# Windowed attention of two heads at a time on the halves of the TensorE array

## The chip, the cores and the metric

The kernel runs on one core of a Trainium2 chip. The metric is the device time of one execution in microseconds (us); smaller is better. TensorE multiplies matrices (its records are PE for the products and PEld for the loading of weights), VectorE is DVE, ScalarE is ACT, GpSimd is POOL, and SyncE (SP) issues most of the DMAs.

## The reference: two layers of a hybrid trunk

The reference runs two layers over 128 context tokens and 1024 sample tokens of 1024 channels. Layer 0 has state-space heads beside long convolutions. Layer 1, which the change touches, is attention with 16 heads of 64 channels. Context tokens attend to all context tokens. The sample is a grid of 16 rows of 64 tokens; each sample token attends to a window of 8 rows by 16 columns with a learned bias, and inside the same softmax to 128 cached keys:

```python
s_loc = jnp.einsum('bhrqd,bhrikd->bhrqik', q, k_rows).astype(jnp.float32) * (HD_C ** -0.5)
...
s_loc = s_loc + bias.transpose(0, 1, 3, 2, 4)[None].astype(jnp.float32)
s_loc = jnp.where(col_in[:, None, :], s_loc, -jnp.inf)
s_ctx = jnp.einsum('bhrqd,bhkd->bhrqk', q, ck).astype(jnp.float32) * (HD_C ** -0.5)
s = jnp.concatenate([s_loc.reshape(b, H_C, R, GRID_W, kh * GRID_W), s_ctx], axis=-1)
p = jax.nn.softmax(s, axis=-1).astype(v.dtype)
...
o = jnp.einsum('bhrqik,bhrikd->bhrqd', p_loc, v_rows) + jnp.einsum('bhrqk,bhkd->bhrqd', p_ctx, cv)
o = o.transpose(0, 2, 3, 1, 4).reshape(b, L, D_C)
return (o * jax.nn.silu(g)) @ w_out
```

## The kernel before

**Foreground and background.** The projections are the foreground: `proj` (L148) multiplies one chunk of 128 output channels with all tokens, in three blocks of 386 columns, each of 8 row blocks times three products (high times high, high times low, low times high: operands are split into a rounded part of type F32R and the rest). `v_proj` (L1164, products L1175 to L1177) does the values with 256 columns. After every block, `tick` (L90) adds `rate` to a credit and lets the background generators in `self.bg` run for as many steps (one step is up to the next `yield`) as the credit allows. In layer 1 the rate is `RA` (L47, 3.9). The time between two ticks is called a slot in the prediction: 24 products of the projection, then the background's steps.

**Order.** `qkv` (L1192) goes over the eight pairs of heads j. It projects the pair's queries `qt` and keys `kt`, for every second j the values of four heads, and puts `attn(j)` into the background. After that come eight chunks of the gates (`silu2`), each multiplied with the attention's output of its pair, and then the output projection (`final`). Semaphores are set by a planner from the data that instructions share. It also orders each engine's and each queue's instructions by when it reckons them ready, so that the order need not be that of the code.

**One attention before** (`attn`, L1258). It loads the cached keys `ck`, the cached values `cv` and the windowed values `vw` (16 DMAs). Then for each of the two heads it makes operands of 128 rows for a head of 64 channels: `Q` holds the queries' rounded part in the head's own 64 rows and the rest in the other 64 (L1285, L1286); `KH` and `KL` hold the keys' rounded part and the rest in the head's own rows (L1290 to L1293) and a copy of them in the other rows (L1294, L1295). So one product of 128 rows with `KH` and one with `KL` (L1320, L1321) give all four products of the parts.

The tiles follow: one tile of 128 context queries for each head, then for each head eight tiles of 128 sample queries (8 grid rows by 16 columns) against 512 keys, four groups of 128. They pass three stages, one stage later with each round of the loop: scores and softmax; the transposition of the four 128 by 128 blocks of weights through TensorE (L1329) and a copy out of PSUM to `Pt` (L1331); the products with the values (L1348), four of them, whose output is 64 channels, and so takes the half of the array's columns, and of the output tile `O`, that belongs to the head. A product of plain f32 operands appears as two records in the trace, a product of F32R operands and a transposition as one. There is a yield after the first and the second stage.

`softmax` (L1240) adds the bias table `Tb` to the scores and finds the maximum in one VectorE instruction (L1251), takes the exponential with its sum on ScalarE (L1253), and divides on VectorE (L1254, L1255). The tables of a head (two tiles of 128 by 3 by 512, one for the upper and one for the lower half of the queries) are loaded by 16 DMAs when the head's first sample tile comes up (`load_tables`, L1155).

**Buffers.** PSUM has five banks for the background (`p_bg`, L198) and three for projections (`p_pj`). `Q`, `KH` and `KL` have two buffers each, `sz` three, `Pt` two, `ck` and `cv` two, `vw` and the tables one.

## Time and profile before

| | us |
|---|---|
| median of 3 runs | 2197.95 (2196.88 to 2198.25) |
| profiled execution, first to last instruction | 2195.9 |
| TensorE busy (products) | 2156.0 |
| VectorE busy | 1423.3 |
| ScalarE busy | 995.3 |
| value products of the attention (L1348), first and last start | 1456.2 and 2067.4 |

The profile is of one execution; the profiler gives its span from the first to the last instruction, and no further time of its own. A row of the trace in order of time gives the start, the duration, the engine, the line, the operation, output and inputs, rows and columns of the array in use (64*128 is 64 rows and 128 columns), the shape that is streamed and how many neighbouring instructions were merged into the row. A row of a list by line gives the number of instructions, their busy time and the mean of one in ns, and behind the second bar the engine's idle time before them with what ended it. Records of TensorE overlap, since products are pipelined: what one costs is the time from its start to the next one's start.

### The profile page before, as it was taken

The numbers are of one execution on the slowest core, as the hardware profiler recorded it, in microseconds if no ns is written. First come the engines' busy times: TensorE is split into PE (matmuls) and PEld (weight loads), VectorE is DVE, ScalarE is ACT, GpSimd is POOL, SyncE is SP. The second block draws the span as 40 slices with busy tenths as digits, with TensorE's granted clock in tenths as the row PEclk, the third lists the DMA queues.
The fourth block names the chain that finished last, engine by engine and source line by source line (L and its number), as shares of the span: only waits on it lengthen the run. The fifth ranks groups of instructions, "written<-read, shape, count | busy, mean of one in ns | idle before, by whom it ended". The sixth has DMA issues, their size and how long they took to land.

```text
span 2195.9 us, 34064 instructions
## 1 busy us (share of the span) xinstructions
PE 2156.0 (98%) x13024; PEld 1937.6 (88%) x13024; DVE 1423.3 (65%) x2948; ACT 995.3 (45%) x2119; POOL 125.4 (6%) x241
## 2 busy tenths in 40 slices
PE   7999999999999999999999999999999999999998
PEld 3899998889999999888878999998888888888877
DVE  5798755546778778987888855734453544555474
ACT  3576544452333232545557303644554544554331
POOL 1110000110000000000000000200000000000000
PEclk9999999999999999999999999999999999999999
DMA  8142255764211122433342521522222223244352
GB/s 322 44 131 98 101 190 179 219 205 156 88 66 63 57 106 86 162 107 119 116 148 96 180 91 49 145 86 60 78 85 81 66 82 94 70 123 126 105 207 78
DMA packets 114947, 256.22 MB, mean 117 GB/s; under 512 B 27048, under 2 KB 63420, under 8 KB 112320
## 3 DMA queue, kind: packets, MB, share of 16 engines
q1 hardware_dynamic: 99472, 191.38, 27.6%
q0 software_dynamic: 15312, 62.67, 8.0%
q8 instruction: 103, 1.69, 0.3%
q14 instruction: 60, 0.48, 0.1%
HBM read 186.61 MB, written 67.38 MB: 116 GB/s over the span
## 4 chain that ended last, share of the span: by engine, by line
PE 58%; issue 2%; DVE 2%; DMA 1%; ACT 1%; POOLq 0%; POOL 0%; SPq 0%; ACTq 0%; DVEq 0%
PE pj L158 9%; PE pj L159 9%; PE pj L160 9%; PE bg L1348 6%; PE bg L1329 3%; PE bg L1320 2%; PE pj L1175 2%; PE pj L1176 2%; PE pj L1177 2%; PE bg L1321 1%; PE bg L1037 1%; PE bg L1005 1%; PE pj L1375 1%; PE pj L1373 1%; PE pj L1374 1%
## 5 line engine op out<-in xcount | busy, mean ns | idle before, releaser
L158 PE MATMUL pj<-hh,whi 128*128 128x386 f32 x1728 | 600.4, 347 | 0.5 <-DVE acc L862 0.5
L159 PE MATMUL pj<-hl,whi 128*128 128x386 f32 x1728 | 591.4, 342 | 0.0
L160 PE MATMUL pj<-hh,wlo 128*128 128x386 f32 x1728 | 588.6, 341 | 0.0
L158 PEld LDWEIGHTS pj<-hh,whi 128*128 128x128 f32 x1728 | 326.4, 189 | 11.5 <-issue 5.7
L159 PEld LDWEIGHTS pj<-hl,whi 128*128 128x128 f32 x1728 | 326.8, 189 | 9.8 <-issue 6.5
L160 PEld LDWEIGHTS pj<-hh,wlo 128*128 128x128 f32 x1728 | 326.6, 189 | 3.5 <-issue 3.1
L131 DVE TENSOR_TENSOR wlo<-wraw,whi 128x1024 fp32r<-128x1024 f32 x108 | 131.9, 1222 | 138.9 <-ACT whi L130 132.1
L130 ACT CAST whi<-wraw 128x1024 fp32r<-128x1024 f32 x108 | 113.0, 1048 | 233.2 <-PE pj L159 225.7
L1251 DVE CUSTOM_DVE_ANT_0 sz<-bg,Tb 128x512 f32<-128x512 f32 x128 | 88.1, 689 | 166.9 <-PE bg L1321 159.6
L598 ACT COPY raw<-pj 128x386 f32<-128x386 f32 x105 | 50.5, 483 | 169.4 <-PE pj L160 82.8
L1331 ACT COPY Pt<-bg 128x512 f32<-128x512 f32 (+1 forms) x144 | 79.0, 549 | 97.1 <-PE bg L1329 95.6
L1253 ACT ACTIVATE sz<-sz,mx 128x512 f32<-128x512 f32 x128 | 92.7, 724 | 53.9 <-DVE mx L1251 53.5
L159 PE MATMUL pj<-ylo,whi 128*128 128x386 f32 x324 | 111.0, 343 | 0.0
L160 PE MATMUL pj<-yhi,wlo 128*128 128x386 f32 x324 | 110.5, 341 | 0.0
L158 PE MATMUL pj<-yhi,whi 128*128 128x386 f32 x324 | 110.4, 341 | 0.0
L1348 PE MATMUL bg<-Pt,vw 128*64 128x128 f32 x768 | 107.8, 277 | 0.0
L1348 PEld LDWEIGHTS bg<-Pt,vw 128*64 128x64 f32 x768 | 84.1, 137 | 11.0 <-issue 8.9
L1175 PE MATMUL pj<-whi,hh 128*128 128x256 f32 x288 | 82.1, 286 | 0.0
L1329 PE MATMUL bg<-csq,sz 128*128 128x128 f32 x528 | 81.6, 273 | 0.2
L1176 PE MATMUL pj<-wlo,hh 128*128 128x256 f32 x288 | 81.2, 282 | 0.0
L1177 PE MATMUL pj<-whi,hl 128*128 128x256 f32 x288 | 80.8, 281 | 0.0
L1329 PEld LDWEIGHTS bg<-csq,sz 128*128 128x128 f32 x528 | 65.1, 140 | 13.6 <-issue 1.8
(428 smaller groups left out, 4457.9 us busy)
## 6 DMA issues: line engine op xcount, KB each, us to landing
wraw<-in_we SPq DMA_DIRECT2D x52, 512.0 KB, 3.9
u<-in_wada SPq DMA_DIRECT2D x34, 512.0 KB, 4.5
wraw<-in_wo SPq DMA_DIRECT2D x24, 512.0 KB, 4.4
Tb<-Cd SPq DMA_DIRECT2D x256, 48.0 KB, 2.0
Hd<-H POOLq DMA_DIRECT2D x8, 1280.0 KB, 5.4
H<-Hd SPq DMA_DIRECT2D x8, 1280.0 KB, 5.4
xt<-xtd SPq DMA_DIRECT2D x17, 512.0 KB, 4.6
wraw<-in_woe SPq DMA_DIRECT2D x16, 512.0 KB, 3.4
```

The lines of the kernel that those rows point to most:

```text
L130: self.nc.scalar.copy(hi, r)
L131: self.nc.vector.tensor_tensor(out=lo, in0=r, in1=hi.bitcast(F32), op=ALU.subtract)
L158: nc.tensor.matmul(p[:, :NB], wh, xh[k][:, sl], start=(k == 0), stop=False)
L159: nc.tensor.matmul(p[:, :NB], wh, xl[k][:, sl], start=False, stop=False)
L160: nc.tensor.matmul(p[:, :NB], wl, xh[k][:, sl], start=False, stop=(k == nk - 1))
L1175: nc.tensor.matmul(p[:, :256], self.hh[k][:, ts], hi[:, q:q + 256], start=(k == 0), stop=False)
L1176: nc.tensor.matmul(p[:, :256], self.hh[k][:, ts], lo[:, q:q + 256], start=False, stop=False)
L1177: nc.tensor.matmul(p[:, :256], self.hl[k][:, ts], hi[:, q:q + 256], start=False, stop=(k == 7))
L1251: V.tensor_tensor_reduce(out=z[:, :n], in0=s, in1=tb, scale=-1.0, scalar=3.0e38, op0=ALU.add, op1=ALU.min, accum_out=mx[:, 1:2])
L1253: nc.scalar.activation(z[:, :n], z[:, :n], AF.Exp, bias=mx[:, 1:2], scale=-1.0, accum_out=mx[:, 2:3])
L1329: nc.tensor.transpose(pt[:, b * 128:(b + 1) * 128], p[:, b * 128:(b + 1) * 128], self.ident)
L1348: nc.tensor.matmul(O[r, cb * 128:(cb + 1) * 128], lv, t[:, b * 128:(b + 1) * 128], start=(b == 0), stop=(b == 3))
```

## The change

Both heads of a pair go through the stages together, so that there are nine rounds of tiles instead of eighteen.

- `QH`, `QL`, `KH`, `KL` hold the rounded parts and the rests of both heads, each head in its own 64 rows. Nothing is copied to the other half. Each has one buffer.
- The scores of a head are three products of 64 rows (QH with KH, QH with KL, QL with KH; the product of the two rests is left out), and the two heads' products alternate between the row halves of the array, into a PSUM bank each.
- The value products of the two heads alternate between the column halves of the array. They now stand ahead of the transposes of the round, without a yield between.
- `softmax` takes both heads: two maxima, two exponentials, one reciprocal for both sums, two scalings. `sz` has four buffers.
- The tables hold both heads, and are loaded at the start of `attn`, behind the loads of `vw`. `ck` and `cv` have one buffer each.
- The output is copied out for both heads in one instruction.
- `RA` is 2.5 instead of 3.9 steps for a slot.

The rest of the diff takes out comments and empty descriptions.

```diff
-    MID, RA = 2, 3.9
+    MID, RA = 2, 2.5
...
-            t = self.t(pool, [128, 3, 512], f"Tb{hf}", bufs=1)
+            t = self.t(pool, [128, 2, 3, 512], f"Tb{hf}", bufs=1)
             c0 = 384 * hf
             V.memset(t, NEG)
-            V.memset(t[:, :, c0:c0 + 128], 0.0)
+            V.memset(t[:, :, :, c0:c0 + 128], 0.0)
...
-    def load_tables(self, h, hf):
+    def load_tables(self, j, hf):
...
-            self.dma(self.Tb[hf][16 * qr:16 * qr + 16, :, 32 * s:32 * s + 256],
-                     self.Cd[:, h, :, 32 * dr:32 * dr + 256].rearrange("a q e -> q a e"))
+            for hh in range(2):
+                self.dma(self.Tb[hf][16 * qr:16 * qr + 16, hh, :, 32 * s:32 * s + 256],
+                         self.Cd[:, 2 * j + hh, :, 32 * dr:32 * dr + 256].rearrange("a q e -> q a e"))
...
+    def softmax(self, ss, tbs, n, pool):
...
+        zs = [self.t(pool, [128, 512], "sz", bufs=4) for s in ss]
+        mx = self.t(pool, [128, 8], "mx", bufs=4)
+        for h, (s, tb, z) in enumerate(zip(ss, tbs, zs)):
+            m1, sm = mx[:, h:h + 1], mx[:, 2 + h:3 + h]
...
+                V.tensor_tensor_reduce(out=z[:, :n], in0=s, in1=tb, scale=-1.0, scalar=3.0e38, op0=ALU.add, op1=ALU.min,
+                                       accum_out=m1)
+                nc.scalar.activation(z[:, :n], z[:, :n], AF.Exp, bias=m1, scale=-1.0, accum_out=sm)
+        V.reciprocal(out=mx[:, 4:6], in_=mx[:, 2:4])
+        for h, z in enumerate(zs):
+            V.tensor_scalar(out=z[:, :n], in0=z[:, :n], scalar1=mx[:, 4 + h:5 + h], scalar2=None, op0=ALU.mult)
+        return zs
...
-        ck = self.t(pool, [128, 256], "ck")
+        R = (slice(0, 64), slice(64, 128))
+        ck = self.t(pool, [128, 256], "ck", bufs=1)
...
-        cv = self.t(pool, [128, 3, 128], "cv")
+        cv = self.t(pool, [128, 3, 128], "cv", bufs=1)
...
+        for hf in range(2):
+            self.load_tables(j, hf)
...
+        QH = self.t(pool, [128, 1024], "QH", F32R, bufs=1)
+        QL = self.t(pool, [128, 1024], "QL", F32R, bufs=1)
+        KH = self.t(pool, [128, 24, 64], "KH", F32R, bufs=1)
+        KL = self.t(pool, [128, 24, 64], "KL", F32R, bufs=1)
+        k, c = kt[:, smp].rearrange("p (r c) -> p r c", c=64), ck.rearrange("p (r c) -> p r c", c=64)
+        for rows, src in ((slice(0, 4), c), (slice(4, 20), k)):
+            nc.scalar.copy(KH[:, rows], src)
+            V.tensor_tensor(out=KL[:, rows], in0=src, in1=KH[:, rows].bitcast(F32), op=ALU.subtract)
+        nc.scalar.copy(KH[:, 20:24], c)
+        V.tensor_copy(KL[:, 20:24], KL[:, 0:4])
+        yield
+        for hf in range(2):
...
+            nc.scalar.copy(qh, q)
+            V.tensor_tensor(out=ql, in0=q, in1=qh.bitcast(F32), op=ALU.subtract)
+        yield
...
-        tiles = [(hh, None, None) for hh in range(2)]
-        tiles += [(hh, hf, cb) for hh in range(2) for hf in range(2) for cb in range(4)]
+        tiles = [None] + [(hf, cb) for hf in range(2) for cb in range(4)]
...
-                    nc.tensor.matmul(s, Q[:, tq], KH[:, kr, kc], start=True, stop=False)
-                    nc.tensor.matmul(s, Q[:, tq], KL[:, kr, kc], start=False, stop=True)
-                    P[i] = self.softmax(s, self.Tb[hf][:, CBT[cb]], 512, pool)
+                    for n, (a, b) in enumerate(((QH, KH), (QH, KL), (QL, KH))):
+                        for r, p in zip(R, s):
+                            nc.tensor.matmul(p, a[r, tq], b[r, kr, kc], start=(n == 0), stop=(n == 2))
+                    P[i] = self.softmax(s, [self.Tb[hf][:, hh, CBT[cb]] for hh in range(2)], 512, pool)
                 yield
...
                     for b in range(4):
-                        lv = cv[:, ROT[cb], r] if b == 3 * hf else vw[:, cb, b + 2 * hf - 1, r]
-                        nc.tensor.matmul(O[r, cb * 128:(cb + 1) * 128], lv, t[:, b * 128:(b + 1) * 128], start=(b == 0), stop=(b == 3))
+                        for r, t in zip(R, ts):
+                            lv = cv[:, ROT[cb], r] if b == 3 * hf else vw[:, cb, b + 2 * hf - 1, r]
+                            nc.tensor.matmul(O[r, cb * 128:(cb + 1) * 128], lv, t[:, b * 128:(b + 1) * 128],
+                                             start=(b == 0), stop=(b == 3))
...
+            if 0 <= i - 1 < len(tiles):
+                nb = 1 if tiles[i - 1] is None else 4
+                Pt[i - 1] = []
+                for p in P.pop(i - 1):
+                    pt = self.ps()
+                    for b in range(nb):
+                        nc.tensor.transpose(pt[:, b * 128:(b + 1) * 128], p[:, b * 128:(b + 1) * 128], self.ident)
+                    t = self.t(pool, [128, 512], "Pt", bufs=2)
+                    nc.scalar.copy(t[:, :nb * 128], pt[:, :nb * 128])
+                    Pt[i - 1].append(t)
+                yield
```

## The prediction

> **What bounds the kernel now.** I read the page's head first, then a stretch of layer 1 by engine, then the chain of waits inside layer 1, then single steps in order of time. Two lines of the page; one of the table by stretches (us, then each engine's busy time, then the clock); the chain's sum by line for 1456 to 2066 us:

> ```profile
> span 2195.9 us, 34064 instructions
> PE 2156.0 (98%) x13024; PEld 1937.6 (88%) x13024; DVE 1423.3 (65%) x2948; ACT 995.3 (45%) x2119; POOL 125.4 (6%) x241
> ```
> ```profile
> 1600.00:1760.00 160.00, 159.90 (x1037) 141.57 (x1036) 74.90 (x191) 80.13 (x167) 5.27 (x8) 1.00 0.28 81
> ```
> ```profile
> by line: PE bg L1348 21.0%; PE pj L158 14.0%; PE pj L159 13.8%; PE pj L160 13.8%; PE bg L1329 9.5%; PE bg L1320 8.6%; PE bg L1321 4.9%; PE pj L1175 4.5%; PE pj L1176 4.2%; PE pj L1177 4.1%; PE bg L1340 0.8%; PE bg L1310 0.8%; issue 0.0%
> ```

> TensorE has no pause in the stage that changes: 159.90 of 160 us, at a granted clock of 1.00, while VectorE and ScalarE are busy for 75 and 80 us. The chain is TensorE alone. Four attention lines (L1348, L1329, L1320, L1321) hold 44.0% of 610 us, 268 us. What shortens TensorE's own sequence shortens the kernel; what is taken from the other engines does not. "Busy" overlaps in these records, so costs are read from start to start. One tile (one head, 128 queries), in order of time:

> ```profile
> 1699.52 0.28 PE L1176 MATMUL pj<-wlo,hh 128*128 128x256 f32 x1
> 1699.64 0.28 PE L1177 MATMUL pj<-whi,hl 128*128 128x256 f32 x1
> 1699.85 0.43 PE L1348 MATMUL bg<-Pt,cv 128*64 128x128 f32 x2
> 1700.12 0.82 PE L1348 MATMUL bg<-Pt,vw 128*64 128x128 f32 x6
> 1700.87 0.51 PE L1320 MATMUL bg<-KH,Q 128*128 128x512 f32 x1
> 1701.21 0.41 PE L1321 MATMUL bg<-KL,Q 128*128 128x512 f32 x1
> 1701.45 0.60 PE L1329 MATMUL bg<-csq,sz 128*128 128x128 f32 x4
> 1701.81 0.36 PE L1175 MATMUL pj<-whi,hh 128*128 128x256 f32 x1
> 1702.01 0.28 PE L1176 MATMUL pj<-wlo,hh 128*128 128x256 f32 x1
> ```

> The value products take 1.02 us (1699.85 to 1700.87; four products, each two records), the scores 0.58 (0.34 + 0.24), the four transposes 0.36. A record of L1348 starts every 0.109 us. The last product of 256 columns is followed after 0.21 us, where the one ahead of it was after 0.12: changing the array's shape costs 0.09 us. The first full-width product after such a change also holds 0.34 us where the next holds 0.24: its successor's weights are not yet in, 0.11 us more. A tile is 1.96 + 0.09 = 2.05 us, a pair of heads **4.10 us**. (The chain gives 268 / 62.5 = 4.3 us a pair; I take the smaller.)

> **Do halves run together?** The trace of before has both kinds. First products on alternating column halves (L1037, the state space's output, same shape as L1348), then row halves (L1310, the context scores):

> ```profile
> 889.18 0.44 PE L1037 MATMUL bg<-ga,xt 128*64 128x128 f32 x4
> 889.55 0.49 PE L1033 MATMUL bg<-csq,yo 128*128 128x128 f32 x2
> ...
> 1188.27 0.66 PE L1037 MATMUL bg<-ga,xt 128*64 128x128 f32 x8
> 1188.86 0.50 PE L1014 MATMUL bg<-Mv,L 128*128 128x512 f32 x1
> ...
> 1677.21 0.49 PE L1310 MATMUL bg<-kt,qt 64*128 64x128 f32 x4
> 1677.63 0.39 PE L1175 MATMUL pj<-whi,hh 128*128 128x256 f32 x1
> ...
> 1758.02 0.34 PE L159 MATMUL pj<-hl,whi 128*128 128x386 f32 x1
> 1758.19 0.34 PE L160 MATMUL pj<-hh,wlo 128*128 128x386 f32 x1
> 1758.46 0.49 PE L1310 MATMUL bg<-kt,qt 64*128 64x128 f32 x2
> 1758.88 0.33 PE L1329 MATMUL bg<-csq,sz 128*128 128x128 f32 x1
> ...
> 1763.97 0.43 PE L1340 MATMUL bg<-Pt,vc 128*64 128x128 f32 x2
> 1764.34 0.51 PE L1320 MATMUL bg<-KH,Q 128*128 128x512 f32 x1
> ```

> Eight records on alternating column halves take 0.59 us to the next shape, four take 0.37; eight on one half took 1.02. So two halves share the time: four records more cost 0.22. And both heads' context scores, four records on both row halves, take 0.42 us (1677.21 to 1677.63), just what one head's two records take (1758.46 to 1758.88). Not shown is a row pair with 512 columns in the rounded type.

> **Part by part, a pair of tiles.**
> Values: 16 records on alternating halves, 0.59 + 2 x 0.22 = 1.03 us in place of 2 x 1.02 (the exit to the next shape is inside both).
> Scores: three products on each row half in place of two full ones a head. Bounds for one step of both halves: below 0.24 (as L1321, shared time), above 0.48 (one after the other). L1310 is the nearest row, so 0.24: 3 x 0.24 + 0.11 for the first weights = 0.83, plus 0.09 to enter.
> Leaving row halves for the values: 0.09 where they follow at once, some 0.29 where a projection stands between; steps are 2.5 to a slot, so 40% are parted: 0.17.
> Transposes: same eight, 0.11 + 8 x 0.109 - 0.08 = 0.90 (the product after them came 0.08 us early above).
> Sum 1.03 + 0.83 + 0.09 + 0.17 + 0.90 = **3.02 us against 4.10**: 1.08 us on each of 64 pairs, 69 us. With the chain's 4.3 it would be 82.
> Context tiles: one paired step of scores (0.42 + 0.09) and one of values (0.37 + 0.09) less for each of 8 attentions, but trace rows like 1677.21 are paired already, so 6 us, not 8.

> [...]

> **Operands and softmax off the path.** Copies to the other half (L1294, L1295) go, the splits run once on 128 partitions. These lists are of 1456 to 2066 us by shape; the memset is of 1380 to 1460.

> ```profile
> L1253 ACT ACTIVATE sz<-sz,mx 128x512 f32<-128x512 f32 x125 | 90.5, 724 | 52.9 <-DVE mx L1251 52.5
> L1251 DVE CUSTOM_DVE_ANT_0 sz<-bg,Tb 128x512 f32<-128x512 f32 x125 | 86.1, 689 | 157.1 <-PE bg L1321 149.8 <-DMA Tb<-Cd 5.3 <-DMA vw<-vd 0.6
> L1331 ACT COPY Pt<-bg 128x512 f32<-128x512 f32 x126 | 73.6, 584 | 94.6 <-PE bg L1329 93.8
> L1255 DVE TENSOR_SCALAR sz<-sz,mx 128x512 f32<-128x512 f32 x125 | 60.7, 486 | 3.5
> L1253 ACT ACTIVATION_READ_ACCUMULATOR sz<-sz,mx 128x1 f32 x125 | 23.5, 188 | 0.0
> L1254 DVE RECIPROCAL mx<-mx 128x1 f32<-128x1 f32 x139 | 22.1, 160 | 43.7 <-ACT sz L1253 40.2 <-ACT sz L1249 3.0
> L1151 DVE MEMSET Tb<- 128x1536 f32 x2 | 2.7, 1338 | 0.7 <-DVE hl L378 0.4 <-issue 0.3
> ```

> These gains cost and give nothing, hidden under TensorE; likewise the doubled memset (2.7 us more on VectorE, once, under the first projection). What could become visible is the chain of a pair's softmax: two maxima (0.69 each), the second exponential done some 2.6 us after the scores (0.69, then two of 0.91), reciprocal 0.16, two scalings of 0.49: 3.7 us. TensorE has values (1.03), transposes (0.90), the next scores (0.9) and again values (1.03) between, 3.9 us, and always at least one slot of projection (24 products x 0.176 = 4.2 us, or 24 x 0.118 = 2.8). So it is covered with some 3 us to spare. Tighter are the two copies to Pt (0.58 each, waiting for the transposes): where values, scores and values fall into one slot, only 0.9 us of scores lie between, against 0.2 + 2 x 0.58 from the last transposes: some 0.5 us is lost, in about one pair of five. With stray cases I charge 8 us. A slot takes 4.2 + 2.5 x 1.5 = 8.0 us for 1.25 pairs, 6.4 a pair; of these VectorE's rows hold 2 x (0.69 + 0.49) + 0.16 = 2.5 and ScalarE's 2 x (0.72 + 0.19 + 0.58) = 3.0, so neither bounds.

> **The slots.** An attention now has 38 steps and its end, 39 / 3.9 = 10.0 slots; after, 21 / 2.5 = 8.4. From the first attention on there are 84 slots (7 x 6 of queries and keys, 3 x 9 x 0.66 of values, 24 of gates); the eight need 67 instead of 80 and sometimes wait a slot for their queries. The projections then run alone at the end; TensorE's sum is the same.

> **The tables' loads** move ahead of the splits. Same number: 16 of vw, 32 of Tb an attention. Their issue on SP and the landing:

> ```profile
> 1746.24 1.71 SPq L84 DMA_DIRECT2D Tb<-Cd  x4
> 1753.50 9.26 SPq L84 DMA_DIRECT2D vw<-vd  x16
> 1762.80 1.83 SPq L84 DMA_DIRECT2D Tb<-Cd  x4
> ```
> ```profile
> DMA to landing us min/median/max: 1.8/2.0/5.8
> ```

> Four Tb loads stand ahead of the vw loads, though the code emits them later: the order on a queue is planned by readiness. The first half table's 16 loads (16 x 0.46 = 7.4 us) can go once half of the last attention is done, so they are hidden; I charge 0, price of the other order below.

> **Sum.** 69 + 6 - 8 = 67 us off the profiled 2195.9: 2129. The runs' median is 2 us above that span: **2131 us**. Own range 2110 (the chain's 4.3 us a pair, no loss) to 2147 (losses three times as large).

> **Rivals.**
> 1. The heads are drawn apart. A pair needs two banks for scores and two for transposes beside one for the output: all five. Where the second head's bank or Pt is ready later, the planner issues one head's products alone, each such pair losing 1.01 us of values and 0.72 of scores. For: the planner does reorder (the Tb loads; 1677.21 pairs two steps that the code keeps apart). Against: TensorE is the late engine, operands wait for it. A third of the pairs: 64 / 3 x 1.73 = 37 us, 2168. Chance 0.13. [...]
> 2. Row halves don't overlap at 512 columns: 3 x 0.24 x 64 = 46 us, 2177. For: no such row. Against: L1310. Chance 0.05.
> 3. Weights of column halves load without overlap, on every step as on a block's first: the block of 889.18 lasts 0.37, of which the last step and the exit take 0.11 + 0.09, the first 0.17. That is 0.06 more on each of eight steps, 8 x 0.06 x 64 = 31 us, 2162. Against: four further records in 0.22. Chance 0.03.
> 4. Slower: the tables come late. If SP issues all vw first (9.3 us), then the first 16 Tb loads (7.4), landing 2.0 later, the first scores' softmax (3.7) ends 22.4 us after the old attention's last values. TensorE reaches the first table pair's transposes after two to three slots and some 3 us, 11 to 16 us. That is 6 to 11 us of waiting in each of 8 attentions; it cancels the gain from 8.4 us each and gives up to 2131 + 88 = 2219. For: the loads now stand behind vw in the code. Against: 1746.24. Chance 0.10, of it 0.02 within the bound.

> **How the numbers follow.** The forecast has 0.69. Faster: 0.69 + 0.13 + 0.05 + 0.03 = 0.90; same 0.02; slower 0.08. About 0.2% (4 us) is what a measurement of this kernel can tell from no change. The range 2106 to 2175 holds the forecast and rivals 1 and 3, and leaves out rival 4, most of 2 and the tails.

> **What would show it.** Right: value records of both heads starting in pairs, 16 in about 1.03 us; score blocks of six in about 0.8; some 75 us less in attention lines of the chain, all else unchanged; the last attention ending well before the last projection. Wrong: VectorE waiting for Tb while TensorE stands; runs of one head's records at 0.109; score records 0.24 apart without a partner.

## The result and the profile after

The changed kernel takes 2131.08 us (median; 2129.30 to 2134.96) against 2198.10 us of the kernel before beside it: a ratio of 0.9695, 95% interval 0.9681 to 0.9709. Timed once more beside later runs it took 2129.68 us, ratio 0.9687 (0.9674 to 0.9701). The forecast was 2131. Beside the experiments below the kernel before took 2197.2 to 2200.2 us, so a difference of up to 3 us between two of them shows little by its median alone.

The page's head, two lines; then the table by stretches (us, each engine's busy time, the clock last but two):

```profile
span 2133.2 us, 34117 instructions
PE 2084.8 (98%) x13152; PEld 1870.8 (88%) x13152; DVE 1355.3 (64%) x2804; ACT 942.2 (44%) x2063; POOL 121.4 (6%) x241
```
```profile
1600.00:1760.00 160.00, 159.92 (x1247) 139.89 (x1246) 68.81 (x185) 79.80 (x183) 4.23 (x7) 1.00 0.30 82
```

TensorE is as full as before, 159.92 of 160 us, but has 1247 records in this stretch where it had 1037 (a pair of tiles has 30 instead of 28): more work goes through in the same time. One pair of tiles, both heads, in the view of TensorE in order of time (start, duration, line, names, array in use, shape, rows merged):

```profile
1552.33 0.28 PE L1179 MATMUL pj<-whi,hl 128*128 128x256 f32 x1
1552.54 0.51 PE L1322 MATMUL bg<-KH,QH 64*128 64x512 f32 x2
1552.89 0.40 PE L1322 MATMUL bg<-KL,QH 64*128 64x512 f32 x2
1553.12 0.40 PE L1322 MATMUL bg<-KH,QL 64*128 64x512 f32 x2
1553.45 0.88 PE L1339 MATMUL bg<-Pt,vw 128*64 128x128 f32 x12
1554.15 0.39 PE L1339 MATMUL bg<-Pt,cv 128*64 128x128 f32 x4
1554.47 1.09 PE L1351 MATMUL bg<-csq,sz 128*128 128x128 f32 x8
1555.32 0.37 PE L1177 MATMUL pj<-whi,hh 128*128 128x256 f32 x1
```

A block, here and below, is a run of records of one line; its time goes from its first start to the start of what follows. Sixteen value records take 1.02 us (1553.45 to 1554.47) where eight took it before. The six score products take 0.91 us (1552.54 to 1553.45), entered 0.21 us after the projection's last product, where the next of its kind would have come after 0.12. The eight transposes take 0.85. From 1552.54 to 1555.32 the pair costs 2.78 us, 2.87 with the entry.

The chain's sum by line, from the second profile of the same kernel (1456 to 1955 us; in the first one a store breaks the chain, see the stops below):

```profile
by line: PE pj L158 15.1%; PE pj L160 14.2%; PE pj L159 14.2%; PE bg L1339 13.1%; PE bg L1351 12.6%; PE bg L1322 11.1%; PE pj L1177 5.6%; PE pj L1178 5.1%; PE pj L1179 5.1%; DMA qt<-gd 1.4%; PE bg L1330 0.6%; PE bg L1313 0.6%; DVE sz L1255 
```

Values, transposes and scores (L1339, L1351, L1322) are 36.8% of 499 us, 184 us for 63 pairs: 2.9 us a pair, where the same lines had 4.3.

**Where the 70 us come from.** Times from each record's start to the next one's, summed over layer 1 by line, from its first projection to the first product of `final`: before 1314.37 to 2082.97, 768.6 us; after 1319.76 to 2018.73, 699.0 us, 69.6 less.

| | before | after | difference |
|---|---|---|---|
| value products | 129.7 | 69.4 | -60.3 |
| scores | 74.4 | 59.5 | -14.9 |
| transposes, without a stop of 3.3 | 62.2 | 61.3 | -0.9 |
| context tiles, without a stop of 2.8 | 11.2 | 5.5 | -5.7 |
| the two stops | 0 | 6.1 | +6.1 |
| projections and the rest | 491.1 | 497.2 | +6.1 |

The profiled run of after lies 5.4 us back when layer 1 begins, in code that is unchanged, and `final` took 1.5 us longer; so the two spans differ by 62.7, while the medians differ by 67.0.

**The other engines wait for TensorE as they did.** VectorE's group of the maxima, 1440 to 1961 us (busy time, mean ns of one, then the idle time before them and what ended it):

```profile
L1255 DVE CUSTOM_DVE_ANT_0 sz<-bg,Tb 128x512 f32<-128x512 f32 x128 | 83.5, 688 | 127.8 <-PE bg L1322 127.2
```

The maximum waits 127.2 us for scores and not at all for `Tb`, which had cost 5.3 us before. The tables still go out ahead of `vw`, though the code has them behind it (SyncE's queue in order of time):

```profile
1560.07 4.19 SPq L84 DMA_DIRECT2D Tb<-Cd  x9
...
1580.87 8.62 SPq L84 DMA_DIRECT2D vw<-vd  x16
```

**Two stops of TensorE that were not foreseen.** TensorE in order of time, with the wait in brackets, and VectorE's row behind the second stop:

```profile
1415.18 0.49 PE L1313 MATMUL bg<-kt,qt 64*128 64x128 f32 x4
1418.21 0.50 PE L1322 MATMUL bg<-KH,QH 64*128 64x512 f32 x2 [2.53 <-ACT QH L1300]
...
1929.34 1.09 PE L1351 MATMUL bg<-csq,sz 128*128 128x128 f32 x8
1933.43 1.25 PE L1322 MATMUL bg<-KH,QH 64*128 64x512 f32 x2 [3.00 <-DVE mx L1255]
...
1936.60 0.53 PE L158 MATMUL pj<-hh,whi 128*128 128x386 f32 x1
1936.92 0.52 PE L159 MATMUL pj<-hl,whi 128*128 128x386 f32 x1
```
```profile
1931.75 1.02 DVE L862 SCALAR_TENSOR_TENSOR gs<-vt,pj 128x386 f32<-128x386 f32 x2 [6.86 <-DMA gd<-gs]
```

The first stop, 2.8 us: the planner puts the first attention's first score products behind three products of the projection of the values and ahead of all the others, and ScalarE has not yet copied the queries. The second, 3.3 us (2.6 in the second profile): the gate's VectorE instruction (L862) waits 6.86 us for the store of the one buffer `gs`; softmax stands behind it in VectorE's order, and the scores need the PSUM bank that softmax reads. Behind it projection products step by 0.32 us (1936.60 to 1936.92) instead of 0.18: the granted clock is 0.50 from 1934.2 to 1937.7 us, as it is from 1418.8 to 1422.2 behind the first stop, where the products of 256 columns step by 0.21 us instead of 0.12.

### The profile page after: what moved, and what is told of

It reads as the page before. It is cut to its first block, busy times and chain, and to the rows that moved or that the text cites. A ratio compares the mean times of both kernels' runs of the same rounds, so it can differ in the third digit from the quotient of the medians.

```text
span 2133.2 us, 34117 instructions
## 1 busy us (share of the span) xinstructions
PE 2084.8 (98%) x13152; PEld 1870.8 (88%) x13152; DVE 1355.3 (64%) x2804; ACT 942.2 (44%) x2063; POOL 121.4 (6%) x241
## 4 chain that ended last, share of the span: by engine, by line
PE 36%; issue 21%; DMA 2%; DVE 2%; ACT 1%; POOL 1%; SPq 0%; POOLq 0%; DVEq 0%; ACTq 0%
PE pj L158 7%; PE pj L159 7%; PE pj L160 7%; PE bg L1037 1%; PE bg L1005 1%; PE pj L1377 1%; PE pj L1376 1%; PE pj L1378 1%; PE bg L1033 1%; PE bg L1014 1%; DMA yr<-yad 1%; PE bg L930 1%; PE bg L1339 1%; PE bg L1351 1%; DMA ycd<-X 1%
## 5 line engine op out<-in xcount | busy, mean ns | idle before, releaser
L158 PE MATMUL pj<-hh,whi 128*128 128x386 f32 x1728 | 603.0, 349 | 0.5 <-DVE acc L862 0.5
L159 PE MATMUL pj<-hl,whi 128*128 128x386 f32 x1728 | 590.2, 342 | 0.0
L160 PE MATMUL pj<-hh,wlo 128*128 128x386 f32 x1728 | 587.6, 340 | 0.0
L158 PEld LDWEIGHTS pj<-hh,whi 128*128 128x128 f32 x1728 | 326.4, 189 | 15.7 <-issue 12.9
L159 PEld LDWEIGHTS pj<-hl,whi 128*128 128x128 f32 x1728 | 326.7, 189 | 7.3 <-issue 6.2
L160 PEld LDWEIGHTS pj<-hh,wlo 128*128 128x128 f32 x1728 | 326.4, 189 | 3.5 <-issue 2.7
L1255 DVE CUSTOM_DVE_ANT_0 sz<-bg,Tb 128x512 f32<-128x512 f32 x128 | 83.5, 688 | 127.8 <-PE bg L1322 127.2
L158 PE MATMUL pj<-yhi,whi 128*128 128x386 f32 x324 | 110.3, 340 | 1.4 <-DVE x L1094 1.4
L159 PE MATMUL pj<-ylo,whi 128*128 128x386 f32 x324 | 110.9, 342 | 0.0
L160 PE MATMUL pj<-yhi,wlo 128*128 128x386 f32 x324 | 110.4, 341 | 0.0
L1353 ACT COPY Pt<-bg 128x512 f32<-128x512 f32 (+1 forms) x144 | 71.9, 549 | 32.4 <-PE bg L1351 28.6
L1177 PE MATMUL pj<-whi,hh 128*128 128x256 f32 x288 | 83.3, 290 | 0.0
L1351 PE MATMUL bg<-csq,sz 128*128 128x128 f32 x528 | 73.9, 280 | 0.0
L923 ACT ACTIVATE xw<-xt,wd 128x64 f32<-128x64 f32 x256 | 64.9, 336 | 14.1 <-PE bg L930 12.0
L1351 PEld LDWEIGHTS bg<-csq,sz 128*128 128x128 f32 x528 | 56.7, 140 | 13.0 <-issue 12.8
L1094 DVE SCALAR_TENSOR_TENSOR x<-pj,mod,x 128x128 f32<-128x128 f32 (+1 forms) x96 | 46.4, 512 | 29.6 <-PE pj L160 25.6
```

Source lines behind the costliest of these rows:

```text
L158: nc.tensor.matmul(p[:, :NB], wh, xh[k][:, sl], start=(k == 0), stop=False)
L159: nc.tensor.matmul(p[:, :NB], wh, xl[k][:, sl], start=False, stop=False)
L160: nc.tensor.matmul(p[:, :NB], wl, xh[k][:, sl], start=False, stop=(k == nk - 1))
L1177: nc.tensor.matmul(p[:, :256], self.hh[k][:, ts], hi[:, q:q + 256], start=(k == 0), stop=False)
L1255: V.tensor_tensor_reduce(out=z[:, :n], in0=s, in1=tb, scale=-1.0, scalar=3.0e38, op0=ALU.add, op1=ALU.min, accum_out=m1)
L1351: nc.tensor.transpose(pt[:, b * 128:(b + 1) * 128], p[:, b * 128:(b + 1) * 128], self.ident)
```

## Experiments: what carries the gain

**Fewer products on the second half** (`e8_one_head_fewer`).

```diff
-                        for r, t in zip(R, ts):
+                        for r, t in list(zip(R, ts))[:2 if b == 0 else 1]:
...
-                                             start=(b == 0), stop=(b == 3))
+                                             start=(b == 0), stop=(b == 3 or r == R[1]))
```

> Three of the second head's four value products are left out (its output holds one group of 128 keys instead of four), so a block has 10 records instead of 16. Theory (a second head's products lie wholly beside the first's): the first head alone took 1.02 us for its eight records, the block stays at 1.0 us, 0 to 3 us less than the changed kernel, 2128 to 2131 us. Rival (each record has its own price, 1.025 / 16 = 0.064 us, and alternating only makes it cheaper): 6 x 0.064 x 64 = 25 us less, 2106 us.

Measured: 2124.23 us (ratio 0.9664, 0.9647 to 0.9680). TensorE in order of time:

```profile
1547.14 0.87 PE L1339 MATMUL bg<-Pt,vw 128*64 128x128 f32 x8
1547.85 0.38 PE L1339 MATMUL bg<-Pt,cv 128*64 128x128 f32 x2
1548.16 1.09 PE L1351 MATMUL bg<-csq,sz 128*128 128x128 f32 x8
```

Ten records take 1.02 us, as sixteen do. Over all blocks the values' sum falls from 69.5 to 67.5 us. The second head's products lie wholly beside the first's; the theory holds. The kernel gained 5 to 7 us, more than the 0 to 3 expected: 2 us are in the values; the second stop was 1.2 us here instead of 3.3 (2.6 in the second profile), but another of 1.0 us came; the rest is not accounted for.

**Scores on all rows** (`e3_scores_full_rows`).

```diff
-                    for n, (a, b) in enumerate(((QH, KH), (QH, KL), (QL, KH))):
-                        for r, p in zip(R, s):
-                            nc.tensor.matmul(p, a[r, tq], b[r, kr, kc], start=(n == 0), stop=(n == 2))
+                    for p in s:
+                        for n, b in enumerate((KH, KL)):
+                            nc.tensor.matmul(p, QH[:, tq], b[:, kr, kc], start=(n == 0), stop=(n == 1))
```

> The scores go back to two products of all 128 rows for each head (QH with KH, QH with KL over the rows of both heads), four in a row for the pair; the three products on row halves and the use of QL are left out, so each score is the sum over both heads' channels. Values stay on alternating column halves. Theory (the gain is that of the values and of fewer separate blocks; the row halves as such bring little): four full steps take 0.34 + 3 x 0.24 = 1.06 us, against 0.91 and 0.09 to enter the row halves: 0.06 us on 64 pairs, 4 us more, range 0 to 8, 2131 to 2139 us. Rival (the row halves carry the scores' gain of 15 us between the two traces): 12 to 15 us more, 2143 to 2146 us.

Measured: 2126.91 us (2120.39 to 2129.99), ratio 0.9667 (0.9646 to 0.9688). TensorE in order of time:

```profile
1549.27 0.28 PE L1179 MATMUL pj<-whi,hl 128*128 128x256 f32 x1
1549.39 0.40 PE L1322 MATMUL bg<-KH,QH 128*128 128x512 f32 x1
...
1550.10 0.40 PE L1322 MATMUL bg<-KL,QH 128*128 128x512 f32 x1
1550.34 0.29 PE L1177 MATMUL pj<-whi,hh 128*128 128x256 f32 x1
```

Four full products take 0.95 us here (1549.39 to 1550.34), against 0.91, but they come 0.12 us after the projection's last product, not 0.21, and the projection's next product follows after 0.24 (1550.10 to 1550.34), as the scores follow each other. Most blocks, 45 of 63, take 1.03 to 1.06 us, since value products of another shape follow. The kernel took 3 to 4 us less than the changed one, where the theory expected 0 to 8 more: the second stop is missing here. Summed over layer 1 the scores take 67.0 us, against 58.4 in `e4_store_from_vt` below, which has no such stop either; in return the projections take 7.2 us less and the transposes 3.8. Layer 1 is equally long in both (692.6 and 692.8 us), the medians are 2.2 us apart. So the row halves as such are worth nothing that shows, and the rival, that they carry the scores' 15 us, falls. By the rows, those come from one block for two tiles: one first step of 0.35 us where the next takes 0.23 (1552.54, 1552.89 and 1553.12 in the changed kernel), and fewer changes of shape, at 0.09 us each (0.21 instead of 0.12). That is the author's estimate; no run tests it alone; nor was a form run that has the operands of before (rests in the other head's rows) for both heads at once.

**Two score products instead of three** (`e7_two_products`).

```diff
-                    for n, (a, b) in enumerate(((QH, KH), (QH, KL), (QL, KH))):
+                    for n, (a, b) in enumerate(((QH, KH), (QH, KL))):
```

> The changed kernel without the third score product (QL with KH) of both heads, so that the queries' rests are left out. Theory (one step of two row halves takes 0.235 us, on TensorE's path throughout): 64 x 0.235 = 15 us less than the changed kernel, 2115 us. Rival (part of TensorE's sequence is slack, so that the attention's own waits take the place): less than 8 us.

Measured: 2114.22 us (ratio 0.9618, 0.9603 to 0.9633), 15 to 17 less than the changed kernel. TensorE in order of time:

```profile
1548.16 0.50 PE L1322 MATMUL bg<-KH,QH 64*128 64x512 f32 x2
1548.50 0.40 PE L1322 MATMUL bg<-KL,QH 64*128 64x512 f32 x2
1548.83 0.38 PE L1177 MATMUL pj<-whi,hh 128*128 128x256 f32 x1
```

The block is 0.67 us instead of 0.91, 0.24 us less on 64 pairs, 15 us: all of it reaches the kernel's time (layer 1 is 14.6 to 15.9 us shorter than in the two profiles of the changed kernel, and the second stop is there, 3.4 us). TensorE's sequence is the path.

## Experiments: must the halves alternate?

**Values head by head** (`e1_values_by_head`).

```diff
-                    for b in range(4):
-                        for r, t in zip(R, ts):
+                    for r, t in zip(R, ts):
+                        for b in range(4):
```

> The value products of a pair of tiles are issued one head after the other (four products of the first, then four of the second) instead of alternating; nothing else differs. Theory (neighbouring records share time only because they lie on different column halves, and only neighbours do): eight records on one half took 1.02 us before, eight more at 0.109 us a step add 0.87 us, so a block goes from 1.025 to about 1.9 us; less the one place where the halves meet. 64 blocks: 50 to 56 us more than the changed kernel, 2181 to 2187 us. Rival (the two halves work off their own products whatever the order of issue): no difference, 2131 us. Second rival (the gain is from fewer shape changes, not from sharing): no difference either, below 4 us.

Measured: 2154.50 us (ratio 0.9798, 0.9783 to 0.9813), 23 to 25 us more: between the theories. One block, TensorE in order of time:

```profile
1555.46 0.93 PE L1339 MATMUL bg<-Pt,vw 128*64 128x128 f32 x8
1556.16 0.27 PE L1339 MATMUL bg<-Pt,cv 128*64 128x128 f32 x1
1556.22 0.27 PE L1339 MATMUL bg<-Pt,vw 128*64 128x128 f32 x1
1556.27 0.27 PE L1339 MATMUL bg<-Pt,cv 128*64 128x128 f32 x1
1556.33 0.49 PE L1339 MATMUL bg<-Pt,vw 128*64 128x128 f32 x3
...
1556.97 1.09 PE L1351 MATMUL bg<-csq,sz 128*128 128x128 f32 x8
```

The block takes 1.51 us, not 1.9. In the program all products of the first head stand ahead of all of the second, and the cached group (`cv`) is the last of each head here. Yet the records mix: `cv` of the first head at 1556.16 and 1556.27 lies between `vw` of the second. Record by record, the first half steps alone by 0.109 us for five records, the fifth at 1555.944; the second half's first starts at 1555.950, while three of the first half are still to come; from there both go on side by side. All 64 blocks do the same. So in these blocks TensorE took a product for the idle half past three records that waited for the busy one, and not while seven to four of them waited. My theory, that only neighbours share time, was wrong in this.

**Scores head by head** (`e2_scores_by_head`).

```diff
-                    for n, (a, b) in enumerate(((QH, KH), (QH, KL), (QL, KH))):
-                        for r, p in zip(R, s):
+                    for r, p in zip(R, s):
+                        for n, (a, b) in enumerate(((QH, KH), (QH, KL), (QL, KH))):
```

> The three score products of the first head are issued ahead of the three of the second instead of alternating between the row halves. Theory (as for the values, only neighbours on different halves share time): the block of six, 0.91 us to the next shape, gets two to three more steps of 0.235 us, 0.47 to 0.70 us, for 64 pairs 30 to 45 us more than the changed kernel, 2161 to 2176 us. Rival (the halves work off their own products): 2131 us.

Measured: 2130.19 us (ratio 0.9688, 0.9673 to 0.9702), no difference. TensorE's instructions of one block as they stand in the program (output and operands with their buffer numbers; bg_13598 is the first head's bank, bg_13599 the second's), and then as they ran:

```
L1322 MATMUL bg_13598<-KH_13383,QH_13381 128x512
L1322 MATMUL bg_13598<-KL_13384,QH_13381 128x512
L1322 MATMUL bg_13598<-KH_13383,QL_13382 128x512
L1322 MATMUL bg_13599<-KH_13383,QH_13381 128x512
L1322 MATMUL bg_13599<-KL_13384,QH_13381 128x512
L1322 MATMUL bg_13599<-KH_13383,QL_13382 128x512
```
```profile
1552.13 0.51 PE L1322 MATMUL bg<-KH,QH 64*128 64x512 f32 x2
1552.47 0.41 PE L1322 MATMUL bg<-KL,QH 64*128 64x512 f32 x2
1552.71 0.40 PE L1322 MATMUL bg<-KH,QL 64*128 64x512 f32 x2
```

The fourth product starts 10 ns after the first (1552.135 and 1552.145), ahead of the second and third. Two waiting products of the other half were no hindrance here; the alternation came by itself. The rival holds here.

**Values by twos** (`e12_values_by_twos`), to tell this from a price that goes with the length of a run.

```diff
-                    for b in range(4):
-                        for r, t in zip(R, ts):
+                    for r, t, b in [(r, t, b + c) for b in (0, 2) for r, t in zip(R, ts) for c in range(2)]:
+                        if True:
```

> The value products alternate by twos: two products of the first head (four records), two of the second, and again. Theory from e1_values_by_head, where the second half's first record started 6 ns behind the fifth of the eight records that stood ahead of it, so with three of them still waiting (TensorE starts a product for an idle half past at most three waiting records): here never more than three wait ahead of the other half's next, so the block stays at 1.03 to 1.08 us, 0 to 3 us more than the changed kernel, 2129 to 2133 us. Rival (only neighbouring products share time, and the cost goes with the length of a run: half of the 0.49 us that e1_values_by_head's blocks were longer): 64 x 0.24 = 15 us more, 2145 us.

Measured: 2132.71 us (2129.11 to 2134.84; ratio 0.9704, 0.9682 to 0.9726). TensorE in order of time:

```profile
1557.85 0.93 PE L1339 MATMUL bg<-Pt,vw 128*64 128x128 f32 x12
1558.55 0.44 PE L1339 MATMUL bg<-Pt,cv 128*64 128x128 f32 x4
1558.92 0.33 PE L1351 MATMUL bg<-csq,sz 128*128 128x128 f32 x1
```

The block takes 1.07 us (1557.85 to 1558.92); the second half starts 14 ns behind the first, although four records stand ahead of it, three of them waiting. Eight of the 64 blocks take 1.50 us, as the second head's copy to `Pt` comes some 0.4 us after the first's there; the values' sum is 73.0 us instead of 69.5. In all three runs the second half's first record started with two or three of the first half's waiting, and in `e1_values_by_head` not while there were more.

## Experiments: the slots' rate and the copies

`e6_ra39` and `e6_ra21` change one number of the changed kernel, `e10_ra30` the same number in `e4_store_from_vt`:

```diff
-    MID, RA = 2, 2.5
+    MID, RA = 2, 3.9
```

> RA back to 3.9 steps a slot, all else as changed. The eight attentions then need 168 / 3.9 = 43 slots instead of 67, and in nearly every slot values, scores and values stand together. Theory of the prediction (the copies to Pt are late in such a slot, 0.5 us each): 40 slots x 0.5 = 20 us more, less 24 entries and exits of slots at 0.2 to 0.3 us, 5 to 7 us: 13 to 15 us more than the changed kernel. Rival (TensorE's order is planned by readiness, other products go between): 5 to 7 us less, for the fewer entries.

Measured: 2138.58 us (ratio 0.9730, 0.9717 to 0.9744), 8.9 more than the changed kernel beside it (2129.68). A block of values in the middle of a slot, TensorE in order of time and then the weight loads with their waits:

```profile
1473.14 0.84 PE L1339 MATMUL bg<-Pt,cv 128*64 128x128 f32 x4
1473.76 0.88 PE L1339 MATMUL bg<-Pt,vw 128*64 128x128 f32 x12
1474.57 0.44 PE L1351 MATMUL bg<-csq,sz 128*128 128x128 f32 x2
```
```profile
1473.14 0.19 PEld L1339 LDWEIGHTS bg<-Pt,cv 128*64 128x64 f32 x2 [0.37 <-ACT Pt L1353]
1473.55 0.19 PEld L1339 LDWEIGHTS bg<-Pt,cv 128*64 128x64 f32 x2 [0.22 <-ACT Pt L1353]
```

The first head's loads wait for its copy to `Pt`, the second head's for the copy after it, 0.41 us later, and the block takes 1.43 us. Sixteen value blocks are longer by 0.4 us, and fifteen score blocks by 0.3 to 0.6 us, since their second bank comes free that much later (in eight of them when VectorE's second maximum, L1255, has read it). The value blocks' loss is the one that the prediction charged (values, scores, values in one slot), at nearly its price, but in 16 blocks and not 40; with 2.5 steps a slot only four value blocks have it, at 0.25 us. The score blocks' loss is another one, which the prediction did not have: the banks. There is no second stop in this run; against `e4_store_from_vt`, which has none either, it is 13.8 us slower.

> RA at 2.1 steps a slot, all else as changed: 80 slots instead of 67, 13 entries and exits more at 0.2 to 0.3 us each, 3 to 4 us; values, scores and values stand in one slot more rarely. Theory of the prediction (0.5 us lost in one pair of five by late copies to Pt): 6 us less for these, 2 to 3 us less in sum. Rival (no such losses at 2.5): 3 to 4 us more than the changed kernel.

Measured: 2135.43 us (ratio 0.9715, 0.9700 to 0.9729), 5.8 more, and not for the number of slots alone. The list of TensorE's waits from 1950 to 1963 us (total, times, longest):

```profile
PE pj L158 <- DVE gs L862: 4.1, 1, 4.1
```

It is the stop of the gates' stage again, moved and longer: with more slots the attentions reach further into that stage. From start to start it holds 4.4 us, where the second profile of the changed kernel has 2.6, so 1.8 us are its. More is in the transposes: without the stops they take 66.7 us instead of 61.4, as 45 of their blocks instead of 26 are followed at once by scores, another change of shape. That is the kind of cost that the rival named (3 to 4 us), though not at the slots' entries; the theory's saving does not show.

> As e4_store_from_vt, with RA at 3.0 steps a slot instead of 2.5: 56 slots instead of 67 for the attentions. Theory from the run with 3.9 (there some 30 blocks were longer by 0.4 to 0.55 us, as one head's products came ahead of the other's, against 24 entries fewer): at 3.0 some slots hold values, scores and values; a third of that, 4 to 5 us more, against 11 entries and exits fewer, 2 to 3 us: 0 to 4 us more than e4_store_from_vt. Rival (fewer entries decide as long as the second head's Pt is in time): 2 to 3 us less.

Measured: 2133.86 us (ratio 0.9707, 0.9692 to 0.9722), 9 us more than `e4_store_from_vt`, more than the 0 to 4 expected. Twelve score blocks are longer by 0.3 to 0.6 us. One of them, the second head's first weight load with its wait:

```profile
1485.09 0.18 PEld L1322 LDWEIGHTS bg<-KH,QH 64*128 64x128 f32 x1 [0.26 <-DVE mx L1255]
```

Four of the twelve wait like this for the bank that VectorE's second maximum still reads; the other eight for a bank that ScalarE's copy of a context tile still reads. The scores take 5.1 us more, the values 2.0 (four blocks are 0.3 to 0.4 us too long, as many as at 2.5 steps) and the transposes 5.0, the projections 2.4 less. And 40 blocks of transposes instead of 26 are followed at once by scores, which costs 0.17 us each: in the trace of the changed kernel the last transposition of a block is followed after 0.20 us by scores and after 0.03 by a projection. So between 2.5 and 3.0 late banks and changes of shape decide; late operands of the value products hardly count.

## Experiments: the two stops

> The changed kernel once more, beside the runs sent with it, as the measure for differences of 0.2%. Every theory expects 2131 us, 2126 to 2134.

Measured: 2129.68 us.

**The store from another buffer** (`e4_store_from_vt`).

```diff
-            nc.vector.scalar_tensor_tensor(out=gs, in0=o, scalar=0.5, in1=gs, op0=ALU.mult, op1=ALU.mult)
+            nc.vector.scalar_tensor_tensor(out=o if j < 7 else gs, in0=o, scalar=0.5, in1=gs, op0=ALU.mult, op1=ALU.mult)
             if j < 7:
-                self.store(self.gd[j], gs)
+                self.store(self.gd[j], o)
```

> In the gates' stage the product with the attention's output is written to the tile that held this output (tag vt, two buffers) and stored from there, instead of into gs, whose one buffer then has to wait for the store. Theory (VectorE waits 44.8 us in 7 times for the store of gs, softmax stands behind it in order, and once, 1930.16 to 1933.43, TensorE stands still for it, then runs some products at half clock): the wait goes to nothing, the stop of 3.3 us goes, and about 1 us of slow products: 3 to 5 us less than the changed kernel. Rival (TensorE only waits there for what would come late anyway, so another wait takes its place, or the stop is of the profiled run alone): within 2 us of the changed kernel.

Measured: 2124.75 us (ratio 0.9664, 0.9650 to 0.9677), 4.9 less. The gate's group on VectorE (1860 to 2020 us) and the stretch 1920 to 1980, first of the changed kernel (second profile), then of this one:

```profile
L862 DVE SCALAR_TENSOR_TENSOR gs<-vt,pj 128x386 f32<-128x386 f32 x24 | 12.9, 553 | 51.6 <-DMA gd<-gs 43.7 <-ACT vt L861 7.9
```
```profile
1920.00:1980.00 60.00, 57.60 (x395) 52.22 (x392) 25.68 (x53) 20.49 (x43) 2.13 (x4) 0.97 0.36 111
```
```profile
L862 DVE SCALAR_TENSOR_TENSOR gs<-vt,pj 128x386 f32<-128x386 f32 x24 | 13.3, 554 | 32.9 <-ACT vt L861 32.9
```
```profile
1920.00:1980.00 60.00, 60.00 (x412) 55.17 (x411) 25.30 (x51) 20.06 (x43) 2.66 (x5) 1.00 0.35 123
```

VectorE's 43.7 us of waiting for the store are gone, TensorE is full (60.00 instead of 57.60), and the granted clock is 1.00 instead of 0.97.

**The first attention a little later** (`e11_first_later`), with the edit above:

```diff
-        ck = self.t(pool, [128, 256], "ck", bufs=1)
+        ck = self.t(pool, [128, T], "vt")[:, 0:256] if j == 0 else self.t(pool, [128, 256], "ck", bufs=1)
```

> As e4_store_from_vt, and the cached keys of the first attention are loaded into a tile of the tag vt, which comes free only while the first values are projected; so TensorE's planned order no longer puts the first attention's score products ahead of that projection. Theory (the stop of 2.8 us at the first attention's scores waits for ScalarE's copy of the queries, and the 17 products after it step by 0.21 instead of 0.12 us): 2.8 + 17 x 0.09 = 4.3 us less than e4_store_from_vt, 2120 to 2122 us. Rival (ScalarE has the same copies to do, so TensorE waits for them elsewhere, or the slow stretch comes all the same): 0 to 2 us less.

Measured: 2120.96 us (ratio 0.9647, 0.9634 to 0.9660), 3.8 less than with the first edit alone; the two ranges overlap by 1.5 us, but in the profiles the stretch from the first product of the value projection to the first of `final` is 595.9 us instead of 599.0. TensorE in order of time; then the stretch 1410 to 1425, of this kernel and of the changed one (second profile):

```profile
1413.13 0.38 PE L1178 MATMUL pj<-wlo,hh 128*128 128x256 f32 x1 [1.11 <-DVE wlo L131]
```
```profile
1410.00:1425.00 15.00, 13.89 (x114) 13.56 (x113) 7.65 (x17) 7.33 (x17) 1.13 (x2) 1.00 0.47 131
```
```profile
1410.00:1425.00 15.00, 12.47 (x83) 11.89 (x82) 9.80 (x19) 7.86 (x17) 1.13 (x2) 0.89 0.52 131
```

Half of the stop stays (1.38 us, a wait for a weight's rest), but the granted clock stays at 1.00 instead of 0.89, and TensorE has 114 products in the stretch instead of 83. Both stops are shown as costs of the changed kernel. With both edits it is the fastest version here that does all the work, 9 us or 0.4% below the changed kernel.

## Why the prediction was right

It said 2131.0 us, from 67 us off the profiled span. Layer 1 became 69.6 us shorter. The mechanism and its largest term were right; that the sum agrees to 0.1 us is luck, since the values gave some 4 us less than forecast, the other attention products about 9 more, and the losses were about 2 larger. By its terms:

- **Values: 64.6 us expected (1.03 us a block in place of 2.04), 60.3 measured.** The block of 1.025 us was right in 52 of 64 cases. Before, the sum was 129.7 and not 130.6; in eight blocks one product of the first head is planned ahead of the others (0.36 + 1.02 us instead of 1.025), and four are 0.25 us longer. That is rival 1 in small: 8 of 64 at 0.36 us, not a third at 1.73. The price was too high for another reason too: an order head by head was partly mended by TensorE itself, wholly in the scores (2130.19 us, no difference) and by 0.4 of 0.87 us in the values (1.51 us a block, not 1.9).
- **Scores, entries and transposes: 4.5 us expected (1.99 us a pair instead of 2.06), about 13 measured** without the losses (scores -14.9, and -1.1 more without the one block at half clock; transposes -0.9; the projections' +6.1 less some 2.6 for slow products behind the stops, so about +3.5, which I put down to the entries). The block of 0.91 us holds the exit, which the working had apart: 0.83 + 0.09 + 0.17 = 1.09 against 0.91 + 0.09 = 1.00. What was too small was the kernel before: the one tile that was read has a projection behind its transposes, which then take 0.36 us, but 91 of the 128 blocks of four take 0.53, since value products of another shape follow, as here in the kernel before:

```profile
1706.40 0.60 PE L1329 MATMUL bg<-csq,sz 128*128 128x128 f32 x4
1706.93 0.87 PE L1348 MATMUL bg<-Pt,vw 128*64 128x128 f32 x6
```

All of them, with the context tiles', took 62.2 us and not 46. So the values, scores and transposes of a pair took 4.16 us before, entries not counted; they lost 76.1 us in the table above, between the 69 and the 82 of the prediction, and 12 came back in the stops and the projections.
- **Context tiles: 6 us, 5.7 measured.**
- **Losses: 8 us charged, about 10 paid, but in another coin.** The step that failed is the late copies to `Pt` in one pair of five at 2.5 steps a slot: there they cost about 1 us, counted with the values above. They are real where the slots are denser (at 3.9 steps 16 blocks, 0.4 us each). What was paid instead are the two stops, 6.1 us, and some 3.7 us of slow products behind them; taking away the second and half of the first brought 4.9 and 3.8 us. Neither was among the rivals: the one comes from the planned order, the other from a buffer outside the lines that the change edits. The second was there in the profile of before, as a group with 11.0 us of waits for that store, and the working did not look at it.
- **Softmax under cover, tables' loads at no cost:** right. VectorE waits for scores only, and no wait for `Tb` is left, so rival 4 fell by the rows of SyncE's queue.
- **Rival 2** fell: the row halves' products start 3 to 4 ns apart at 512 columns, and a step of both takes 0.24 us.
- **Rival 3** fell: no step of the values is longer than with one half (0.16 us for the first, then 0.109, as before), and ten and sixteen records take the same 1.02 us.
- **The slots:** the last value product came at 1961 us, with 55 us of projections behind it, as said. That the rate leaves TensorE's sum the same was wrong: 2.1, 3.0 and 3.9 steps cost 6 to 9 us, through late copies and banks, changes of shape and the gate's store.

## What to carry to other kernels

Where an engine's own sequence is the path, look for products that use half of its rows or columns and put two of them in flight on different halves: the second was free here (sixteen records in 1.02 us, where one half's eight took it), and alternating by ones or twos was enough (1.02 and 1.07 us a block). Reckon the gain from sums over the stage, not from one tile, and put the stalls in a row of their own. After such a gain look for the new stops where the shortened stage now meets the next one: a single buffer and its store, which did not stop TensorE before, cost 4.9 us here.

## What the runs showed of the hardware

The second stop cost more than its length: the 3.3 us were followed by products at 0.32 us a step instead of 0.18, at a granted clock of 0.50 for 3.4 us, and the run without the stop (`e4_store_from_vt`) was 4.9 us faster. Behind the stop of 1.4 us that `e11_first_later` keeps, the clock stayed at 1.00.
